# Making the second pair's operands in four stretches of the first pair instead of two

## The chip, the core and the metric

One program runs on 1 core of one Trainium2 chip. The metric is device time in microseconds (us) of that core, the median of repeated runs.

## The reference

One layer of a decoder trunk on 2048 tokens and 1024 features: a mixer (gated linear attention beside RWKV-7) added to the residual stream, then a channel mixer, then a final norm. The change lies in the channel mixer, `x2` being the residual stream after the mixer:

```python
h = modulate(x2, norm_ffn_g, sh_f, sc_f)         # rms norm, scale, shift
u = h @ w_up                                     # 1024 -> 2 * 2816
u = sum(conv_w[j] * up[:, j:j + T] for j in range(3)) + conv_b   # up: u with two zero rows ahead
gate, val = split(u, 2)
x = x2 + gt_f * ((silu(gate) * val) @ w_down)    # 2816 -> 1024
```

## The kernel before

The tokens are cut into four blocks of 512, and the channel mixer takes them in two pairs (`hs[0]`, `hs[1]`; loop variable `e`). The up projection of a pair goes over 22 tiles `j` of 128 gate features and the 128 value features beside them. A Strassen-Winograd scheme makes the four products of a tile out of seven smaller ones: seven `Up` slots a tile (`what` 1 to 7), each with 4 x 3 matmuls of 128x128 by 128x512 (L1296 to L1298; three, because each fp32 operand is carried as a rounded high part and a low part).

The moving operands of a pair are sums and differences of modulated quarters, named b11, b21, b22, t1 to t4, four tiles each. They are made once, written to DRAM (`opd`), and read back by `Feed`. For pair 0 that happens in the phase before. For pair 1 it happens while pair 0 runs its up tiles, in `made_ahead`:

- `operand_row` makes the row of inverse norms of a block with 4 small transposing matmuls (L1063) and one ScalarE copy (L1064).
- `operand_one(e, k)`, k = 0 to 3, loads two tiles of x2 (L1069), and its `rest` scales them (`op_scale`: VectorE L1073, ScalarE L1074) and stores b11 and b21 from ScalarE's queue (L1083).
- `operand_two(e, k)` loads two tiles of x2 and the b11 and b21 just stored. Its `rest` has two `op_scale`, two GpSimd subtractions (L1096, L1098), two VectorE operations (L1100, L1102), one store on ScalarE's queue (L1095) and four on SyncE's (L1097, L1099, L1101, L1103).

A step of `made_ahead` first runs the `rest` of the step before it and then issues its own loads; a last step, `None`, only runs the open `rest`. So `rest` of k runs one step after the loads of k. The tiles lie in a pool of five buffers (`acct`, tag "xt") that the down projection's accumulator tiles share.

Everything stands in one list of slots, which `run` goes through. A slot's weights are loaded six slots ahead and split into high and low part (`parts_of`: ScalarE L1217, then L1218 in turn on VectorE and GpSimd) three slots ahead; an `Other` slot counts in both distances. After each slot one background function is run: the convolution (`conv`, VectorE L1327 and L1328) and the gate (`hidden`, VectorE L1336, L1337, L1340) of the tile before. The matmuls of the down projection (`Down`, L1353 to L1355) come after every four up tiles, in 16 slots that stand behind slots 1 and 2 of tiles 3, 7, 11, 15, 19.

So PE runs in turn a stretch of 28 up slots (the last five of one tile, three whole tiles, the first two of the next) and a stretch of 16 down slots. The up stretches of pair 0 are called here S1 (tiles 4 to 6 whole), S2 (8 to 10), S3 (12 to 14) and S4 (16 to 18). Tile's scheduler gives each engine its fixed order at build time, from the program's order and a simulated clock; every engine then works through its queue in that order.

Of the kernel before, what the change touches and what calls it, by code (L numbers as in the profile page):

```python
# [95 lines left out]
def hybrid_kernel(ctx, tc, x, cst, vec, c_row, ada_t, w_in, w_v, w_first, w_z, gk_up, wa_up, g_up,  # L96
# [177 lines left out]
    step = [0]  # L274
# [235 lines left out]
    slots = (("rw_bk", 1), ("rw_rbk", 2), ("rw_rbk", 2), ("gl_g", 1), ("gl_vt", 1))  # L510
# [548 lines left out]
    def operand_row(b, at):  # L1059

        ps = pools["norm"]()
        for t in range(4):
            PE.matmul(out=ps[:, t * P:(t + 1) * P], lhsT=rn2[:, b, t:t + 1].broadcast_to([P, P]), rhs=ident, start=True, stop=True)  # L1063
        A.copy(out=at, in_=ps)  # L1064
        op_r[b] = at
# [170 lines left out]
    def bg_step():  # L1236
        if bg:
            bg.pop(0)()
        elif idle:
            idle.pop(0)()  # L1240
# [184 lines left out]
    def finish_later(b, sums):  # L1425
        r, rb = lp.tile([P, 4], F32, name="rn3", tag="rn3", bufs=2), []

        def norm():
            with tc.issue_after(state["last"]):
                rstd_tok(r, sum_tok(sums))  # L1430

        def rows():
            with tc.issue_after(state["last"]):
                rb.append(spread(up, r))

        def nothing():
            pass

        idle.extend([nothing] * 3 + [norm] + [nothing] * 2 + [rows])
        idle.extend(lambda ft=ft: finish_tile(b, ft, rb[0]) for ft in range(KT))  # L1440
# [3 lines left out]
    def down_slots(e, g, hid, sums=None, feed=()):  # L1444
        slots = []
        for ft in range(KT):
            shared = {}
            slots += [Down(e * HB + i, i, ft, g, hid, shared, sums, feed[ft * HB + i:ft * HB + i + 1]) for i in range(HB)]
        return slots
# [4 lines left out]
    def last_block():  # L1454

        wait = [Feed(0, n_, k, hs[0], cvt) for n_ in ("t2", "t3", "t1") for k in range(4)]
        gen = []

        def begin():
            at = iter(["b22"] * 4 + ["t4"] * 4)  # L1460
            pools["pair"] = lambda: hc(next(at))
            gen.append(stage_d(NBLK - 1, prep_d(NBLK - 1), lp.tile([P, NB], F32, name="d_ss", tag="fs", bufs=HB)))
            for f in wait[:2]:
                f.load()

        def one(ft):
            next(gen[0], None)
            for f in wait[2 * ft:2 * ft + 2]:
                f.split()
            for f in wait[2 * ft + 2:2 * ft + 4]:  # L1470
                f.load()

        def end():
            with tc.issue_after(state["last"]):
                for _ in gen[0]:
                    pass

        return [Other(begin)] + [Other(lambda ft=ft: one(ft)) for ft in range(KT)], Other(end)

    def made_ahead(e):  # L1480

        open_ = []

        def step(f):
            for r in open_:
                r()
            open_[:] = [f()] if f is not None else []

        def first(f, b):
            with tc.issue_after(state["last"]):  # L1490
                operand_row(b, up.tile([P, NB], F32, name="rbc", tag="ns", bufs=1))
            return f()

        zones = []
        for i, f in enumerate((operand_one, operand_two)):
            fs = [lambda k=k, f=f: f(e, k) for k in range(4)]
            fs[0] = lambda g=fs[0], b=2 * e + i: first(g, b)
            zones.append([Other(lambda f=f: step(f)) for f in fs + [None]])
        return zones

    hs = [{} for _ in range(NBLK // HB)]
# [4 lines left out]
    slots = []  # L1506

    def U(e, j, what, *feed):
        slots.append(Up(j, what, us[e][j], hs[e], hids[e][group_of[j]], feed))

    def feeds(e, n_, place):
        return [Feed(e, n_, k, hs[e], place) for k in range(4)]

    def begin(e):
        U(e, 0, 1, *feeds(e, "b11", acct if e else ubt))
        U(e, 0, 2, *feeds(e, "b21", acct if e else ubt))
        U(e, 1, 1)

    def stage_e(e):
        if e == 0:  # L1520
            begin(0)
            work, end = last_block()
            slots.extend(work)
        U(e, 0, 6)
        U(e, 1, 2)
        U(e, 0, 7)
        if e == 0:
            slots.append(end)
        U(e, 0, 5)
        U(e, 0, 3, *(feeds(e, "b22", acct) if e == 0 else ()))  # L1530
        U(e, 1, 6)
        U(e, 0, 4, *feeds(e, "t4", acct))
        U(e, 1, 7)
        U(e, 1, 5)
        more = e + 1 < len(hs)
        zones = made_ahead(e + 1) if more else [[], []]
        for j in range(2, NH):
            aside = zones[0] if 4 <= j < 7 else zones[1] if 8 <= j < 11 else []
            U(e, j, 1)
            U(e, j, 2)  # L1540
            if j > 1 and group_of[j - 2] != group_of[j - 1]:
                slots.extend(down_slots(e, group_of[j - 2], hids[e][group_of[j - 2]]))
            U(e, j - 1, 3)
            U(e, j, 6)
            if aside:
                slots.append(aside.pop(0))
            U(e, j - 1, 4)
            U(e, j, 7)
            U(e, j, 5)
            if aside:  # L1550
                slots.append(aside.pop(0))
        U(e, NH - 1, 3)
        U(e, NH - 1, 4)
        if more:

            begin(e + 1)
            last = kgroups[-1]

            def flush():
                while bg:  # L1560
                    bg_step()
                sums[e][:] = [lp.tile([P, NB], F32, name="x_ss", tag="fs", bufs=HB) for _ in range(HB)]

            sums[e] = []
            slots.append(Other(flush))
            fs = [f for n_ in ("t2", "t3", "t1", "b22") for f in feeds(e + 1, n_, ubt)]
            slots.extend(down_slots(e, last, hids[e][last], sums[e], fs))

            def later():
                for i in range(HB):  # L1570
                    finish_later(e * HB + i, sums[e][i])

            slots.append(Other(later))
# [3 lines left out]
    for e in range(len(hs)):  # L1577
        stage_e(e)
# [101 lines left out]
```

## Time and profile before

| | us |
|---|---|
| median of 3 runs | 2907.91 (2906.29 to 2908.95) |
| the profiled execution | 2900.88 |
| its span, first to last instruction | 2899.1 |
| PE / DVE / ACT / POOL busy | 95% / 71% / 45% / 38% of the span |

The profiled execution is one run; its own time is 1.8 us above its span. PE is TensorE's matmuls and PEld its weight loads, DVE is VectorE, ACT is ScalarE, POOL is GpSimd, SPq is SyncE's queue of DMA issues. Names in rows are those of the kernel's tiles; L1218 is line 1218. Matmuls overlap in the engine's pipe, so what one costs is read from the distance of starts.

### The profile page before, as it was taken

To read this page: it belongs to the slowest core of one execution; us is meant where nothing else is said; L and a number is where in the kernel's file an instruction comes from. 1 tells how busy PE (TensorE), PEld (TensorE's weight loads), DVE (VectorE), ACT (ScalarE), POOL (GpSimd) and SP (SyncE) were. 2 spreads that over 40 slices of the span, in tenths; PEclk is the share of its full clock that TensorE was granted. 3 is DMA by queue.
4 is the path that set the end of the run, shared out by engine and by line. 5 is a ranking of instruction groups with operands and counts; after the bars stand their busy time and mean duration, and the time that the engine had idled before them with its cause. 6 is when DMAs were issued, how large, how long until landed. Compare 5 with 4: busy or idle time off the path is not lost.

```text
span 2899.1 us, 54969 instructions
## 1 busy us (share of the span) xinstructions
PE 2745.4 (95%) x20296; PEld 2224.0 (77%) x20296; DVE 2058.9 (71%) x4090; ACT 1309.7 (45%) x2737; POOL 1087.6 (38%) x1147
## 2 busy tenths in 40 slices
PE   6989999999999999999899998999999899999997
PEld 5778777877787877777677786888878678888887
DVE  8357877766766667867557868668597777595777
ACT  4445335444454445554343534435264344253443
POOL 5224212312221223322345545536336545363441
PEclk9999989999999998988899999999999999999999
DMA  8988955545555566664875446442544734425243
GB/s 287 336 286 307 313 166 171 175 135 162 171 173 155 167 185 192 208 191 153 287 262 167 131 155 198 130 141 88 164 155 156 246 123 127 142 83 165 88 135 105
DMA packets 381965, 520.49 MB, mean 180 GB/s; under 512 B 82816, under 2 KB 155776, under 8 KB 381696
## 3 DMA queue, kind: packets, MB, share of 16 engines
q1 hardware_dynamic: 342960, 475.02, 51.4%
q10 hardware_dynamic: 38736, 41.95, 4.2%
q8 instruction: 160, 2.62, 0.4%
q14 instruction: 109, 0.89, 0.1%
HBM read 361.65 MB, written 155.19 MB: 178 GB/s over the span
## 4 chain that ended last, share of the span: by engine, by line
PE 39%; DVE 8%; DMA 5%; issue 2%; ACT 1%; POOL 1%; SPq 0%; DVEq 0%; ACTq 0%; POOLq 0%
PE g_bank L1298 7%; PE g_bank L1296 7%; PE g_bank L1297 7%; PE g_bank L1353 5%; PE g_bank L1354 5%; PE g_bank L1355 5%; DVE cv L1327 1%; DMA acc<-acc 1%; DVE cv L1328 1%; DVE w_lo L1218 1%; PE g_bank L283 1%; PE g_bank L282 1%; PE g_bank L281 1%; DVE acc L1422 1%; DMA mx<-mix 1%
## 5 line engine op out<-in xcount | busy, mean ns | idle before, releaser
L1298 PE MATMUL g_bank<-h_hi,w_lo 128*128 128x512 f32 x1232 | 479.7, 394 | 16.6 <-DVE w_lo L1218 14.2
L1296 PE MATMUL g_bank<-h_hi,w_hi 128*128 128x512 f32 x1232 | 484.8, 394 | 9.2 <-ACT w_hi L1217 4.2
L1297 PE MATMUL g_bank<-h_lo,w_hi 128*128 128x512 f32 x1232 | 484.1, 393 | 0.0
L1217 ACT CAST w_hi<-w_st 128x512 fp32r<-128x512 f32 (+1 forms) x396 | 238.1, 607 | 466.7 <-PE g_bank L1354 326.5
L1356 DVE SCALAR_TENSOR_TENSOR acc<-g_bank,mod,acc 128x512 f32<-128x512 f32 (+1 forms) x200 | 144.2, 728 | 236.1 <-PE g_bank L1355 216.8
L1218 POOL TENSOR_TENSOR w_lo<-w_st,w_hi 128x512 fp32r<-128x512 f32 x154 | 224.6, 1459 | 221.3 <-ACT w_hi L1217 220.7
L281 PE MATMUL g_bank<-h_hi,w_hi 128*128 128x512 f32 x736 | 299.8, 408 | 3.2 <-DVE rn L243 2.2
L283 PE MATMUL g_bank<-h_hi,w_lo 128*128 128x512 f32 x736 | 295.5, 402 | 0.0
L282 PE MATMUL g_bank<-h_lo,w_hi 128*128 128x512 f32 x736 | 295.4, 402 | 0.0
L1298 PEld LDWEIGHTS g_bank<-h_hi,w_lo 128*128 128x128 f32 x1232 | 234.0, 190 | 72.4 <-DVE w_lo L1218 19.4
L1296 PEld LDWEIGHTS g_bank<-h_hi,w_hi 128*128 128x128 f32 x1232 | 234.1, 190 | 62.4 <-ACT w_hi L1217 9.4
L1297 PEld LDWEIGHTS g_bank<-h_lo,w_hi 128*128 128x128 f32 x1232 | 233.9, 190 | 48.7
L1353 PE MATMUL g_bank<-hh,w_hi 128*128 128x512 f32 x640 | 251.9, 397 | 9.2 <-DVE acc L1356 7.2
L1354 PE MATMUL g_bank<-hl,w_hi 128*128 128x512 f32 x640 | 251.2, 394 | 0.0
L1355 PE MATMUL g_bank<-hh,w_lo 128*128 128x512 f32 x640 | 251.2, 394 | 0.0
L1218 DVE TENSOR_TENSOR w_lo<-w_st,w_hi 128x512 fp32r<-128x512 f32 (+1 forms) x242 | 193.9, 801 | 21.3 <-ACT w_hi L1217 21.1
L281 PEld LDWEIGHTS g_bank<-h_hi,w_hi 128*128 128x128 f32 x736 | 140.6, 191 | 37.0 <-DVE rn L243 3.0
L283 PEld LDWEIGHTS g_bank<-h_hi,w_lo 128*128 128x128 f32 x736 | 140.4, 191 | 31.5 <-DMA w_lo<-klo 1.0
L282 PEld LDWEIGHTS g_bank<-h_lo,w_hi 128*128 128x128 f32 x736 | 140.8, 191 | 28.0
L1353 PEld LDWEIGHTS g_bank<-hh,w_hi 128*128 128x128 f32 x640 | 119.6, 187 | 43.3 <-DVE acc L1356 9.9
L1355 PEld LDWEIGHTS g_bank<-hh,w_lo 128*128 128x128 f32 x640 | 119.8, 187 | 29.5
L1354 PEld LDWEIGHTS g_bank<-hl,w_hi 128*128 128x128 f32 x640 | 119.8, 187 | 28.9 <-DVE hl L1340 0.3
(352 smaller groups left out, 6096.4 us busy)
## 6 DMA issues: line engine op xcount, KB each, us to landing
acc<-acc SPq DMA_DIRECT2D x352, 256.0 KB, 3.1
w_hi<-khi SPq DMA_DIRECT2D x188, 256.0 KB, 3.4
w_lo<-klo SPq DMA_DIRECT2D x188, 256.0 KB, 3.7
w_st<-in_ffn_up SPq DMA_DIRECT2D x176, 256.0 KB, 3.0
w_st<-in_ffn_down SPq DMA_DIRECT2D x80, 256.0 KB, 2.8
khi<-w_hi ACTq DMA_DIRECT2D x68, 256.0 KB, 4.0
klo<-w_lo SPq DMA_DIRECT2D x68, 256.0 KB, 4.0
w_st<-in_ada_t SPq DMA_DIRECT2D x64, 256.0 KB, 4.6
```

Source lines behind the costliest of these rows:

```text
L281: PE.matmul(out=ps, lhsT=wh, rhs=hi, start=k == 0, stop=False)
L282: PE.matmul(out=ps, lhsT=wh, rhs=lo, start=False, stop=False)
L283: PE.matmul(out=ps, lhsT=wl, rhs=hi, start=False, stop=k == KT - 1)
L1217: A.copy(out=hi, in_=t)
L1218: eng.tensor_tensor(out=lo, in0=t, in1=hi.bitcast(F32), op=ALU.subtract)
L1296: PE.matmul(out=ps, lhsT=wh[:, c], rhs=hi, start=first and k == 0, stop=False, skip_group_check=True)
L1297: PE.matmul(out=ps, lhsT=wh[:, c], rhs=lo, start=False, stop=False, skip_group_check=True)
L1298: state["last"] = PE.matmul(out=ps, lhsT=wl[:, c], rhs=hi, start=False, stop=last and k == 3, skip_group_check=True).ins
L1353: PE.matmul(out=ps, lhsT=wh, rhs=hh, start=j == 0, stop=False)
L1354: PE.matmul(out=ps, lhsT=wh, rhs=hl, start=False, stop=False)
L1355: PE.matmul(out=ps, lhsT=wl, rhs=hh, start=False, stop=j == n - 1)
L1356: V.scalar_tensor_tensor(out=a_, in0=ps, scalar=mod[:, 40 + ft:41 + ft], in1=a_, op0=ALU.mult, op1=ALU.add)
```

## The change

`made_ahead` now gives four lists of steps in place of two: each operand's four `k` are cut into two halves, each with its own closing `None`. In the loop over tiles, one step a tile is taken, behind slot 6 of the tile before slot 4, in tiles 4, 5, 6 (operand one, k = 0 and 1), 8, 9, 10 (operand one, k = 2 and 3), 12, 13, 14 (operand two, k = 0 and 1) and 16, 17, 18 (operand two, k = 2 and 3). Before, two steps a tile were taken, behind slot 6 and behind slot 5: operand one in tiles 4, 5 and once in 6, operand two in 8, 9 and once in 10.

```diff
         for i, f in enumerate((operand_one, operand_two)):
             fs = [lambda k=k, f=f: f(e, k) for k in range(4)]
             fs[0] = lambda g=fs[0], b=2 * e + i: first(g, b)
-            zones.append([Other(lambda f=f: step(f)) for f in fs + [None]])
+            zones += [[Other(lambda f=f: step(f)) for f in part + [None]] for part in (fs[:2], fs[2:])]
         return zones
...
-        zones = made_ahead(e + 1) if more else [[], []]
+        zones = made_ahead(e + 1) if more else []
         for j in range(2, NH):
-            aside = zones[0] if 4 <= j < 7 else zones[1] if 8 <= j < 11 else []
+
+            aside = zones[j // 4 - 1] if zones and j >= 4 and j % 4 != 3 and j < 20 else []
...
             U(e, j, 5)
-            if aside:
-                slots.append(aside.pop(0))
```

## Rows read from the trace of the kernel before

**Rows 1.** The page's line of busy time, share and instructions of each engine.

```profile
PE 2745.4 (95%) x20296; PEld 2224.0 (77%) x20296; DVE 2058.9 (71%) x4090; ACT 1309.7 (45%) x2737; POOL 1087.6 (38%) x1147
```

**Rows 2.** Windows S1, S2, S3, S4: length, PE, PEld, DVE, ACT, POOL busy, clock, DMA, GB/s.

```profile
1577.00:1656.00 79.00, 75.53 (x331) 60.80 (x331) 71.56 (x88) 47.77 (x80) 49.79 (x45) 1.00 0.43 140
...
1701.00:1793.00 92.00, 83.53 (x348) 67.29 (x347) 84.87 (x94) 49.05 (x82) 63.67 (x55) 0.94 0.54 173
...
1837.00:1914.00 77.00, 77.00 (x341) 63.72 (x340) 69.14 (x84) 46.72 (x77) 49.63 (x48) 1.00 0.28 91
...
1958.00:2035.00 77.00, 76.75 (x339) 63.23 (x338) 68.63 (x81) 45.16 (x75) 46.09 (x48) 1.00 0.27 86
```

**Rows 3.** PE's timeline: first matmul of S2, first down matmul behind it; the same for S3.

```profile
1701.26 0.39 PE L1296 MATMUL g_bank<-h_hi,w_hi 128*128 128x512 f32 x1
...
1792.57 0.39 PE L1353 MATMUL g_bank<-hh,w_hi 128*128 128x512 f32 x1
...
1837.37 0.39 PE L1296 MATMUL g_bank<-h_hi,w_hi 128*128 128x512 f32 x1
...
1913.55 0.39 PE L1353 MATMUL g_bank<-hh,w_hi 128*128 128x512 f32 x1
```

**Rows 4.** PE's waits with their releasers, on the timeline: first in S1, two in S2.

```profile
1623.25 0.50 PE L1298 MATMUL g_bank<-h_hi,w_lo 128*128 128x512 f32 x1 [0.60 <-DVE w_lo L1218]
...
1750.13 0.50 PE L1298 MATMUL g_bank<-h_hi,w_lo 128*128 128x512 f32 x1 [1.07 <-DVE w_lo L1218]
...
1771.11 0.80 PE L1298 MATMUL g_bank<-h_hi,w_lo 128*128 128x512 f32 x1 [3.83 <-DVE w_lo L1218]
```

**Rows 5.** PE's waits in S2 (first row) and S4, in total: us, times, longest.

```profile
PE g_bank L1298 <- DVE w_lo L1218: 7.6, 3, 3.8
...
PE g_bank L1298 <- POOL w_lo L1218: 0.3, 1, 0.3
```

**Rows 6.** Windows of 4 us in S2, columns as in rows 2: the clock falls.

```profile
1753.00:1757.00 4.00, 3.42 (x14) 2.55 (x14) 4.00 (x4) 1.05 (x3) 4.00 (x4) 1.00 0.63 217
1757.00:1761.00 4.00, 1.29 (x4) 1.04 (x4) 4.00 (x3) 0.00 (x0) 3.85 (x3) 0.86 0.31 112
1761.00:1765.00 4.00, 4.00 (x14) 3.14 (x14) 3.65 (x5) 3.48 (x6) 2.27 (x3) 0.72 0.90 310
...
1773.00:1777.00 4.00, 4.00 (x11) 3.13 (x10) 4.00 (x7) 2.18 (x4) 2.44 (x2) 0.51 0.91 284
```

**Rows 7.** Groups by line: L1073 in S1; then S2's VectorE and GpSimd work of operand two.

```profile
L1073 DVE SCALAR_TENSOR_TENSOR acc<-acc,mod,rbc 128x512 f32<-128x512 f32 x8 | 7.4, 969 | 1.3 <-DMA acc<-x 1.3
...
L1073 DVE SCALAR_TENSOR_TENSOR acc<-acc,mod,rbc 128x512 f32<-128x512 f32 x8 | 8.9, 1126 | 0.0
...
L1100 DVE SCALAR_TENSOR_TENSOR acc<-acc 128x512 f32<-128x512 f32 x4 | 3.8, 950 | 1.2 <-POOL acc L1098 1.2
L1102 DVE SCALAR_TENSOR_TENSOR acc<-acc 128x512 f32<-128x512 f32 x4 | 3.8, 948 | 0.0
...
L1096 POOL TENSOR_TENSOR acc<-acc 128x512 f32<-128x512 f32 x4 | 6.7, 1667 | 4.8 <-ACT acc L1074 2.0 <-DMA acc<-op_b 1.8 <-PE g_bank L1298 1.0
L1098 POOL TENSOR_TENSOR acc<-acc 128x512 f32<-128x512 f32 x4 | 6.6, 1647 | 0.0
```

**Rows 8.** VectorE's timeline in S2: operand two's operations up to the first PE wait.

```profile
1730.71 2.06 DVE L1073 SCALAR_TENSOR_TENSOR acc<-acc,mod,rbc 128x512 f32<-128x512 f32 x3
...
1736.34 1.77 DVE L1100 SCALAR_TENSOR_TENSOR acc<-acc 128x512 f32<-128x512 f32 x1 [1.19 <-POOL acc L1098]
...
1740.02 0.68 DVE L1102 SCALAR_TENSOR_TENSOR acc<-acc 128x512 f32<-128x512 f32 x1
...
1744.31 1.77 DVE L1073 SCALAR_TENSOR_TENSOR acc<-acc,mod,rbc 128x512 f32<-128x512 f32 x1
```

**Rows 9.** The small matmuls of a row of inverse norms, PE's timeline, in S2.

```profile
1726.21 1.05 PE L1063 MATMUL rj_bank<-ident,rn 128*128 128x128 f32 x8
```

**Rows 10.** SyncE's queue: a wait in S2's end; first read of pair 1's operands.

```profile
SPq L1374 <- DMA op_t<-acc: 3.2, 2, 2.9
...
2083.07 1.39 SPq L1249 DMA_DIRECT2D acc<-op_b  x2
```

## The prediction

> **What bounds the kernel now.** I read the busy line first: PE is busy 95% of the span, so a gain can only come from time in which PE stands still or runs slowly [rows 1]. Then I cut pair 0 into its stretches. Without steps, in S3, 28 up slots last 1913.55 - 1837.37 = 76.2 us, or 2.72 a slot and 19.05 a tile. S2, the same slots with all of operand two, lasts 1792.57 - 1701.26 = 91.3 us [rows 3]. The windows show the same: PE is never idle in S3, idle 0.25 us in S4, 3.5 us in S1 (79 - 75.53), 8.5 us in S2 (92 - 83.53), where the granted clock is also only 0.94 on average [rows 2]. The reader should see DVE beside it: 85 of 92 us busy in S2, 72 of 79 in S1, and still 69 of 77 where no step runs. The waits say how this reaches PE: in S2, 7.6 us are for `w_lo`, the low half of a weight, made by DVE [rows 5]. DVE takes its queue in order, so a split stands behind the operands' work; it is put there three slots (8.2 us) before PE needs it, or two real slots (5.4 us) where an `Other` slot lies between. When DVE is later than this, PE stops. In S2 the clock also falls after such stops, to 0.51 in one window, which is the lower of its two levels (1.2 GHz of 2.4) [rows 6].
>
> **The change part by part.** No operation is added or dropped; 8 executions of `rest` change place, with their 24 loads and 28 stores.
>
> *What S2 gives back.* 91.3 - 76.2 = 15.1 us. The small matmuls of a row (at most 1.05 us [rows 9]) move with operand two to S3, so about 14.1 us is stall. It splits into 8.5 us idle and 0.06 x 92 = 5.5 us of clock [rows 2], which sums to 14.0. All of it is operand two's: S3 has everything else and no loss.
>
> *What S1 gives back.* 3.5 us [rows 2].
>
> *Two halves of operand one, now in S1 and S2.* A whole one is 8 DVE operations, 7.4 us [rows 7]; a half is 3.7 us, in two lots of 1.85, a tile apart. How much can DVE take before PE stops? In S1 PE first waited at 1623 us, after all 7.4 us; in S2 at 1749 us, after the first six operations, 2.06 + 1.77 + 0.68 + 1.77 = 6.3 us [rows 4, 8]. So some 6 us are carried by the lead of the splits, and 3.7 lies below it. Price 0; the upper bound is half of S1's loss each, 3.5 us together.
>
> *Two halves of operand two, now in S3 and S4.* In S2 the 16 DVE operations took 8.9 + 3.8 + 3.8 = 16.5 us and the 8 GpSimd ones 6.7 + 6.6 = 13.3 us [rows 7]: 4.1 and 3.3 us for one `rest`. The two of a half come 43.5 and 62.6 us into the stretch (16 and 23 slots of 2.72), 19 us apart. DVE has 77 - 69.1 = 7.9 us to spare in S3 and 8.4 in S4 [rows 2], so about 2 us a tile. At the second `rest` its lag is 4.1 - 2.0 + 4.1 = 6.2 us, just at the 6 us. To this may come the hold on GpSimd: L1100 waits for L1098, 1.2 us in the one case where DVE had no backlog [rows 7, 8]. Now most cases will be of that kind, 1.2 us a `rest`, and the lag becomes 8.6 us. So 0.2 to 2.6 us of stall a stretch from this side; S4 idles 0.25 us for a late split before anything is added, so there is no margin below [rows 2, 5], and I take 2.5 each, 5 in all. Bounds: 0 and half of what S2 loses each, 14.1 together. Behind S3 and S4 come down stretches, in which DVE has little to do and catches up.
>
> *Queues.* SyncE's queue gets the same loads and stores, in other stretches. DMA is busy 0.54 of S2, and only 0.28 and 0.27 of S3 and S4 [rows 2]: price 0. What is late next would be the x2 tiles: operand two holds four of the five "xt" buffers, now for a tile's length. The down slots need them at the end of S3 and S4, and the last `rest` stands in the same place ahead of them (slot 6 of the third tile) as in S2 now, where SyncE's wait for these stores came to 3.2 us [rows 10] and PE went on into the down matmuls at 1792.57 without a gap. Price 0. The later end is no trouble: the last `rest` would run at about 1958 + 63 = 2021 us, and the first read of these operands was issued at 2083 [rows 10].
>
> *Slots.* Slots behind slot 5 vanish from four tiles and six tiles of S3 and S4 get one; each shortens the lead of a split by 2.72 us while it lies between. That is part of the two bounds above. The empty list for pair 1 changes nothing.
>
> **A rule against the change.** Rows first: in S2 GpSimd worked 63.7 us against 49.6 in S3, yet DVE's other work took 84.9 - 16.5 = 68.4 us there and 69.1 in S3 [rows 2, 7]; 13 us more of GpSimd made the rest of DVE's work no longer. The Trainium skill, "SBUF — State Buffer", section "Who interferes with whom", says that a VectorE instruction with two SBUF inputs and a GpSimd one that reads SBUF exclude each other, the second blocking until the first is done. By that rule the subtractions would cost DVE time in S3 and S4 that spreading doesn't save; the rows just read don't show it.
>
> **The sum.** 14.1 + 3.5 - 5.0 = 12.6 us. From the profiled execution's 2900.9 us that gives 2888.3. That run lies 7.0 us under the median of the timed ones and below the fastest of them, so I put the same difference on the median: 2907.9 - 12.6 = 2895.3, say 2895.
>
> **The rivals.**
>
> *The stall goes along with the work (no change).* S1 lost 3.5 us on 7.4 us of added DVE time, 0.47 of it; S2 lost 14.1 on 16.5 + 13.3 = 29.8 us of DVE and GpSimd time, again 0.47. If that share is lost wherever the work is put, S1 to S4 lose 17.6 us as before: 2907.9. Against it: PE's waits begin only after 6 to 7 us have been added [rows 4, 8], which is a threshold and no share, and the clock's 5.5 us need long stops (3.8 us was the longest [rows 5]). For it: DVE is 90% busy in S3 and S4 without any step. If half of it were true the gain would be 9 us.
>
> *GpSimd's subtractions block DVE (slower).* In each of S3 and S4 DVE gets 8.2 us of its own and loses 6.6 us to the two pairs of subtractions, 14.8 in all, and has 7.9 and 8.4 us to take them: 6.9 + 6.4 = 13.3 us lost, and with stops of that length the clock's 5.5 us in both, 11. So 24.3 us against 17.6 saved: 2914.6. It decides once S3 and S4 lose over 11.7 us each (17.6 + 5.8, halved). For it: DVE operations of 0.7 us stretch to 1.77 beside GpSimd [rows 8]. Against it: S2's DVE sum, above. This is where that rule of the Trainium skill would lead.
>
> *The steps don't spread.* The order on each engine is fixed by the scheduler's clock and not by the program alone; if it draws the steps together, little changes: 2907.
>
> **How the numbers follow.** Forecast, S3 and S4 together losing 0 to 10 us: 0.68, with 2890 to 2900. Stall in proportion: 0.20, of which a quarter keeps a gain over 5.8 us and a tenth turns slower. Blocking: 0.08. No spreading: 0.04. Changes of 0.2% (5.8 us) are about what a measurement of this kernel can tell from none. So faster 0.68 + 0.05 = 0.73, same 0.13 + 0.04 = 0.17, slower 0.10. The 8-in-10 range starts at the price of nothing in S3 and S4, 2907.9 - 17.6 = 2890.3, less a microsecond of scatter, 2889, and goes up into the proportional case, to 2907.
>
> **What would show it.** Right: four up stretches of 77 to 80 us; DVE some 73 us busy in S1 and S2 and 77 in S3 and S4; PE without a wait in S1 and S2 and with 1 to 4 us in each of S3 and S4, for DVE's `w_lo`; a granted clock of 1.00 in all four. Wrong: S3 and S4 of 84 us and more with a fallen clock (proportion or blocking; in the blocking case DVE's other work is longer than 69 us), `rest` of two k close together, or a gap ahead of the down stretches with SyncE waiting for stores of the operands.

## The result, and the profile after

The changed kernel takes 2916.87 us (median of 17 executions; one of 5232.72 us stands apart, the others lie between 2909.70 and 2926.24). The kernel before, run beside it, takes 2901.56 (17 executions, 2893.22 to 2908.95). The ratio is 1.0051, 95% interval 1.0041 to 1.0062: the change costs 12 to 18 us. Forecast were 2895, with a range of 2889 to 2907, and a gain of 12.6; the result lies above the range, and the sign was wrong.

The profiled execution took 2920.11 us, its span 2918.3, which is 19.2 more than the span before. The page's busy line shows the same work as in [rows 1]:

```profile
PE 2750.0 (94%) x20296; PEld 2227.0 (76%) x20296; DVE 2066.5 (71%) x4090; ACT 1306.2 (45%) x2737; POOL 1087.2 (37%) x1147
```

The stretches S1 to S4, cut at the first up and the first down matmul of each, columns as in [rows 2]:

```profile
1581.67:1657.82 76.15, 73.61 (x321) 60.52 (x320) 71.90 (x87) 45.97 (x79) 50.09 (x46) 0.98 0.35 114
1702.62:1788.00 85.38, 79.30 (x338) 64.37 (x336) 72.59 (x86) 47.13 (x79) 46.98 (x48) 0.96 0.31 102
1832.80:1919.50 86.70, 80.08 (x345) 64.72 (x344) 78.26 (x92) 48.45 (x82) 57.26 (x52) 0.98 0.41 135
1964.30:2054.44 90.14, 80.89 (x338) 65.06 (x336) 77.22 (x93) 47.55 (x81) 57.31 (x52) 0.94 0.39 128
```

Two of S1's 28 slots run among the small down slots ahead of it, so S1 as cut here holds 26 and its length can't be set beside those of the others. S1 starts 1.9 us later than before (1579.82) and is 0.5 shorter; S2 falls from 91.3 only to 85.4, S3 grows from 76.2 to 86.7, S4 from 76.7 to 90.1. The four stretches sum to +17.5, and with the later start that is the whole difference of the two spans. S3 has VectorE's late splits, as the prediction named them, only more of them (6.2 us below). S2 and S4 are the odd ones. S2 holds half of operand one, which was priced at nothing; DVE is just as busy there as forecast (72.6 against "some 73"), and yet PE stands still for 6.1 us. So VectorE's load isn't the matter there. The waits (us, times, longest) say what is; PE, ACT and DVE in S2 first, then SyncE's queue from 1690 to 1716, then PE in S3 and in S4:

```profile
PE g_bank L1296 <- ACT ub L1305: 4.1, 1, 4.1
PE g_bank L1298 <- POOL w_lo L1218: 1.9, 1, 1.9
...
ACT acc L1074 <- DVE acc L1073: 13.7, 3, 8.4
...
DVE acc L1073 <- DMA acc<-x: 11.5, 4, 6.7
...
SPq L1069 <- DMA acc<-acc: 4.7, 3, 2.2
SPq L1069 <- DMA op_b<-acc: 3.5, 1, 3.5
...
PE g_bank L1298 <- DVE w_lo L1218: 6.2, 3, 2.6
...
PE g_bank L1298 <- DVE w_lo L1218: 3.8, 1, 3.8
PE g_bank L1298 <- POOL w_lo L1218: 2.7, 3, 1.8
PE g_bank L1296 <- ACT ub L1305: 2.7, 1, 2.7
```

VectorE stands 11.5 us for loads of x2, a wait that came to 1.3 us in S1 before [rows 7]; ScalarE stands 13.7 us behind VectorE; and PE waits 4.1 us for a copy that ScalarE makes (`ub`, L1305). SyncE's queue, which issues the loads (L1069), stands 4.7 us for the down slots' stores, whose buffers the loads fill, and 3.5 for a store of an operand made just before. The timeline at the start of S2 shows the chain link by link (SyncE's issues, VectorE, ScalarE, PE; the bracket is the idle time before and its releaser):

```profile
1698.52 0.38 SPq L1382 DMA_DIRECT2D acc<-acc  x1
...
1701.66 0.32 SPq L1069 DMA_DIRECT2D acc<-x  x1
...
1705.23 0.96 SPq L1069 DMA_DIRECT2D acc<-x  x2
1706.67 0.32 SPq L1382 DMA_DIRECT2D acc<-acc  x1
1710.54 0.32 SPq L1069 DMA_DIRECT2D acc<-x  x1
...
1704.66 1.33 DVE L1073 SCALAR_TENSOR_TENSOR acc<-acc,mod,rbc 128x512 f32<-128x512 f32 x1 [6.68 <-DMA acc<-x]
...
1714.23 0.75 DVE L1073 SCALAR_TENSOR_TENSOR acc<-acc,mod,rbc 128x512 f32<-128x512 f32 x1 [2.88 <-DMA acc<-x]
...
1706.02 0.73 ACT L1074 ACTIVATE acc<-acc,mod 128x512 f32<-128x512 f32 x1 [8.41 <-DVE acc L1073]
...
1715.02 0.72 ACT L1074 ACTIVATE acc<-acc,mod 128x512 f32<-128x512 f32 x1 [2.92 <-DVE acc L1073]
1715.65 0.57 ACT L1305 COPY ub<-g_bank 128x512 f32<-128x512 f32 x1
...
1717.47 0.58 ACT L1305 COPY ub<-g_bank 128x512 f32<-128x512 f32 x1
...
1713.58 0.39 PE L1298 MATMUL g_bank<-h_hi,w_lo 128*128 128x512 f32 x1
1718.10 0.79 PE L1296 MATMUL g_bank<-h_hi,w_hi 128*128 128x512 f32 x1 [4.14 <-ACT ub L1305]
```

A step's load (L1069) is issued among the stores of the down slots (L1382) whose "xt" buffers it fills. VectorE's L1073 waits for it, ScalarE's L1074 for that, and behind L1074 stand two copies out of PSUM, for the second of which PE stops behind the matmul of 1713.58. The loads of this step are hung on slot 6 of tile 8 and its `rest` on that of tile 9, within S2, which begins at 1702.62; on the chip the first load is issued at 1701.66, and VectorE stands at the `rest` from 1697.98 on (1704.66 - 6.68).

Why it is early shows in the order that the scheduler gave VectorE. Of VectorE's queue only the operands' operations and two markers are listed, from the start of S1 (u: an up slot's L1309; d: a down slot's L1356, d14 and d16 so many of them; O: L1073; P: L1100 or L1102). Added are three kernels of the experiments:

```
before    uuuOOOOOuOOuOuuuuuuu d16 uuuOOOuPPuOuOPPOuOPuPOuOPPuuu d16 uuuuuuuuuuuu d16 uuuuuuuuuuuu
after     uuuOOOOuuuuuuuuu d14OdOOdO uuuuuuuuuuuu d16 uuuOOOuPPuOuPPuuuuuu d14OdOdPPOO uPuPuuuuuuuuuu
e1_row    uuuOOOOuuuuuuuuu d16 uuuOOOOuuuuuuuuu d16 uuuOOOuPPuOuPPuuuuuu d16 uuuOOOuPPuOuPPuuuuuu
e2_pin    uuuuuuOOuuuOOuuu d16 uuuuuuOOuuuOOuuu d16 uuuuuuOOuPPuuOOPPuuu d16 uuuuuuOOuPPuuOOPPuuu
e4_unpin  OOOuOOOOuOuuuuuuuuuu d14OdOdPPOOuOPuPOuOuPPOuPuPuuuuuu d16 uuuuuuuuuuuu d16 uuuuuuuuuuuu
```

In the changed kernel the steps of S2 and S4 begin between the last two down slots, ahead of the stretch. Only the first step of an operand has something that holds it: `first` makes the row of inverse norms inside `tc.issue_after(state["last"])`, and every L1073 behind it reads that row. The second halves, k = 2 and 3, find the row ready, and the scheduler draws them as far forward as its clock allows. Also, the two `rest` of a half stand together (OOOO) and not a tile apart.

### The profile page after: what moved, and what is told of

Its sections match the earlier page's. It is cut to its first block, busy times and chain, and to the rows that moved or that the text cites. A ratio compares the mean times of both kernels' runs of the same rounds, so it can differ in the third digit from the quotient of the medians.

```text
span 2918.3 us, 54965 instructions
## 1 busy us (share of the span) xinstructions
PE 2750.0 (94%) x20296; PEld 2227.0 (76%) x20296; DVE 2066.5 (71%) x4090; ACT 1306.2 (45%) x2737; POOL 1087.2 (37%) x1147
## 4 chain that ended last, share of the span: by engine, by line
PE 36%; DVE 10%; DMA 6%; issue 2%; ACT 1%; POOL 1%; SPq 0%; DVEq 0%; ACTq 0%; POOLq 0%
PE g_bank L1298 7%; PE g_bank L1296 7%; PE g_bank L1297 7%; PE g_bank L1353 4%; PE g_bank L1355 4%; PE g_bank L1354 4%; DVE cv L1327 2%; DMA acc<-acc 1%; DVE cv L1328 1%; DMA acc<-x 1%; DVE w_lo L1218 1%; DVE hl L1340 1%; DVE acc L1422 1%; DVE th L1337 1%; PE g_bank L282 1%
## 5 line engine op out<-in xcount | busy, mean ns | idle before, releaser
L1296 PE MATMUL g_bank<-h_hi,w_hi 128*128 128x512 f32 x1232 | 485.8, 395 | 13.7 <-ACT ub L1305 7.1
L1217 ACT CAST w_hi<-w_st 128x512 fp32r<-128x512 f32 (+1 forms) x396 | 237.1, 606 | 450.6 <-PE g_bank L1354 333.3
L1356 DVE SCALAR_TENSOR_TENSOR acc<-g_bank,mod,acc 128x512 f32<-128x512 f32 (+1 forms) x200 | 144.3, 728 | 234.4 <-PE g_bank L1355 214.2
```

The source lines that it names most:

```text
L1217: A.copy(out=hi, in_=t)
L1296: PE.matmul(out=ps, lhsT=wh[:, c], rhs=hi, start=first and k == 0, stop=False, skip_group_check=True)
L1356: V.scalar_tensor_tensor(out=a_, in0=ps, scalar=mod[:, 40 + ft:41 + ft], in1=a_, op0=ALU.mult, op1=ALU.add)
```

## The experiments

All times are medians in us, each with the kernel before run on the same chip (2900.3 to 2902.2, beside e13 and e14 2906.4). The last column is the time from the start of S1 to the end of S4 in the one profiled execution, 455.25 for before and 472.77 for after; what lies outside those stretches varies between the profiled executions by some 20 us (2432 to 2453) and isn't in it.

| kernel | median (range) | ratio to before, 95% | S1 to S4 |
|---|---|---|---|
| e1_row | 2907.62 (2900.61 to 2917.61) | 1.0019, 1.0006 to 1.0033 | 459.30 |
| e2_pin | 2901.48 (2887.71 to 2909.92) | 1.0001, 0.9986 to 1.0015 | 454.55 |
| e4_unpin | 2907.70 (2904.86 to 2922.28) | 1.0032, 1.0019 to 1.0045 | 469.12 |
| e7_none | 2876.44 (2871.59 to 2879.42) | 0.9918, 0.9905 to 0.9931 | 436.08 |
| e3_bpin | 2903.19 (2896.93 to 2909.51) | 1.0006, 0.9991 to 1.0020 | 459.74 |
| e12_nosub | 2902.14 (2893.85 to 2912.17) | 0.9996, 0.9981 to 1.0010 | 452.54 |
| e10_slots | 2878.13 (2871.38 to 2885.80) | 0.9932, 0.9915 to 0.9948 | 437.10 |
| e9_noslot | 2896.28 (2886.61 to 2905.16) | 0.9990, 0.9975 to 1.0004 | 456.49 |
| e8_stage | 2888.84 (2881.48 to 2890.48) | 0.9967, 0.9954 to 0.9979 | 447.04 |
| e13_mul | 2891.71 (2881.68 to 2896.81) | 0.9945, 0.9925 to 0.9966 | 446.06 |
| e14_muladd | 2889.82 (2881.86 to 2900.25) | 0.9942, 0.9920 to 0.9963 | 445.40 |
| e15_pin3 | 2890.76 (2884.68 to 2895.23) | 0.9968, 0.9953 to 0.9983 | 447.52 |
| e16_cutv | 2899.04 (2887.75 to 2904.32) | 0.9992, 0.9977 to 1.0008 | 453.49 |
| e6_down | 2882.30 (2877.55 to 2892.46) | 0.9950, 0.9932 to 0.9967 | 442.99 |

### Is it the hold that the second halves lack?

**e1_row** gives k = 2 a row of its own, made again:

```diff
             fs[0] = lambda g=fs[0], b=2 * e + i: first(g, b)
+            fs[2] = lambda g=fs[2], b=2 * e + i: first(g, b)
```

> The changed kernel, with a row of inverse norms made afresh ahead of the third step of each operand too, so that all four half lists begin behind a matmul of their own place. Theory A (a half list without a fresh row is drawn by the scheduler into the down stretch ahead, and VectorE then waits for tiles that wait for buffers): no wait of L1073 for a load of x in S2 and S4, S2 falls from 85.4 us to about 81 and S4 from 90.1 to about 87, the whole to about 2909 (2904 to 2912), still not under the kernel before, since two steps still run in a bunch behind each row. Theory B (a fixed share of the added VectorE and GpSimd time is lost wherever it is put): no change from 2917, or slower by the two rows, 2 us.

It came to 2907.62. In the order above no step stands between down slots any more, and in the trace VectorE's L1073 waits for no load. The windows of S2 and S4:

```profile
1695.62:1775.06 79.44, 77.78 (x346) 63.65 (x345) 71.34 (x84) 47.77 (x80) 49.54 (x47) 1.00 0.35 110
...
1950.89:2035.58 84.69, 79.95 (x346) 64.77 (x345) 75.24 (x88) 47.42 (x80) 53.39 (x51) 0.98 0.42 134
```

S2 is 5.9 shorter, S4 5.5, S3 stays (86.23). So about 9 of the 15 us come from the missing hold (ratios 1.0051 and 1.0019).

**e4_unpin** takes the hold away in the kernel before:

```diff
-            with tc.issue_after(state["last"]):
-                operand_row(b, up.tile([P, NB], F32, name="rbc", tag="ns", bufs=1))
+            operand_row(b, up.tile([P, NB], F32, name="rbc", tag="ns", bufs=1))
```

> The kernel before, with the row of inverse norms made without being queued behind the last matmul (the two-stretch lists are as they were). Theory A: without that hold operand two goes into the end of the down stretch and VectorE waits there for x as in the changed kernel's S2 and S4, 10 us or so in all; S2 at 95 us or more, the whole slower than before by 5 to 15 us, 2911. Theory B: as before, 2901.6.

It is 0.32% slower (5.5 us), at the low end of theory A's range. Operand two now begins in the down stretch, and S2 takes 99.2 us against 91.3:

```profile
1708.85:1808.08 99.23, 83.68 (x338) 65.77 (x336) 86.54 (x101) 49.96 (x85) 63.05 (x56) 0.93 0.50 164
```

Giving the hold to the one kernel and taking it from the other moves both the way that this cause demands.

### What would the change bring if the steps stood where they are hung?

**e2_pin** holds each `rest` behind VectorE's last L1309 (`lastv`):

```diff
         def step(f):
             for r in open_:
-                r()
+                with tc.issue_after(state["lastv"]):
+                    r()
```

> The changed kernel, with each rest issued on VectorE behind the last L1309 of its own slot, so that one step a tile is what the queue really has. No operation is added. Theory A: no wait of L1073 for x, S1 and S2 at 77 to 78 us, S3 and S4 at 78 to 82, the whole at 2892 (2888 to 2898), faster than the kernel before: the place of the steps was right and the queue did not have it. Theory B: 2917 as the changed kernel, or 2901 as the one before, since the same work is added to the same stretches.

The order is now the one the prediction spoke of (OO, a tile, OO), and it is 15 us faster than the changed kernel. But it takes 2901.48, the same as before: the gain that the spread was expected to bring (2892) isn't there.

**e3_bpin** is the kernel before with the same hold, so two stretches with two steps a tile.

> The kernel before, two stretches and two steps a tile, with every rest pinned behind VectorE's last L1309, as in e2_pin. Theory E (spreading over four stretches has a worth of its own once the steps stay where they are hung): two stretches take what e2_pin's four take, but in bunches, so this one is slower than e2_pin's 2901.5 by 5 us or more: about 2908, with S2 at 90 us or more. Theory F (each step costs what it costs, some 25 us over the twelve, wherever it stands): 2899 to 2904, the same as before and as e2_pin, with S1 at 75 and S2 at 91.

2903.19 lies in theory F's range and 5 us under theory E's number. Its S2 takes 84.9, where theory E said 90 or more and theory F 91, and its S1 to S4 are 5.2 us longer than e2_pin's in the one execution of each. The medians differ by 1.7 us with intervals that overlap. Held in this way, four stretches are at best worth a few us more than two, not the 12.6 that were forecast.

**e7_none** measures what there is to gain: pair 1's operands aren't made at all.

```diff
-            nc.sync.dma_start(out=self.t, in_=opd[self.e][self.n_][self.k])
+            nc.sync.dma_start(out=self.t, in_=opd[0][self.n_][self.k])
...
-        zones = made_ahead(e + 1) if more else [[], []]
+        zones = [[], []]
```

> The kernel before without making the second pair's operands at all: the second pair reads the first pair's from DRAM, so its outputs are the first pair's products; all loads, matmuls and the rest stay. This is the floor for any placing of the steps. Both theories: S1 to S4 at 76.2 us each, the whole 17.6 us under the kernel before, 2884 (2881 to 2887). If it is well above, part of the stalls in S1 and S2 has another cause than the steps.

2876.44. The steps cost the kernel before 20 to 28 us by the interval, not the 17.6 of the prediction; S1 to S4 show 19.2 of it. The stretches without them:

```profile
1576.88:1647.62 70.74, 70.74 (x314) 58.58 (x313) 64.73 (x80) 42.36 (x72) 46.10 (x44) 1.00 0.27 86
1692.42:1769.26 76.84, 76.48 (x337) 62.98 (x336) 68.91 (x81) 45.11 (x75) 47.42 (x48) 1.00 0.27 86
1814.06:1890.97 76.91, 76.52 (x338) 63.00 (x336) 68.77 (x81) 45.02 (x75) 46.51 (x48) 1.00 0.27 85
1935.77:2012.96 77.19, 76.47 (x337) 63.01 (x336) 69.90 (x81) 45.13 (x75) 47.67 (x48) 1.00 0.27 86
```

A row's small matmuls take PE 0.8 us of these differences (from the first of them at 1599.34 to the next matmul at 1600.14 in S1 before). S2's loss of 14.1 was read rightly (91.3 - 76.8 - 0.8 = 13.7). S1 loses 5.1 (76.6 - 70.7 - 0.8) and not 3.5: only PE's idle time had been read there, since no stretch of its kind without steps was at hand.

### What takes the time in the spread kernel?

First the rival of the prediction. **e12_nosub** is e2_pin without the two subtractions on GpSimd for pair 1:

```diff
-            G.tensor_tensor(out=b11, in0=b11, in1=b12, op=ALU.subtract)
+            if e == 0: G.tensor_tensor(out=b11, in0=b11, in1=b12, op=ALU.subtract)
```

(and the same for L1098).

> e2_pin without GpSimd's two subtractions in pair 1's operand two (L1096, L1098 left out, so t1 to t4 of pair 1 hold other values). Theory G (GpSimd's subtractions hold VectorE up, the rival of the prediction): S3 and S4 lose their 13.3 us of it and their clock loss, down from 83 and 82 to 77 to 78 each, so 2901.5 - 11 = 2890 or less. Theory H (the steps cost through ScalarE's wait for L1073 and VectorE's own queue; GpSimd's work lies beside): S3 and S4 fall by 0 to 3 us each, 2896 to 2901, and S1 and S2 stay.

2902.14 against 2901.48: no gain, with intervals of about 4 us to either side, where theory G wanted 11 us. S3 and S4 fall by 1.9 and 0.6 us, to 81.4 and 81.7, not to 77 or 78. Theory G falls as it was priced; the median lies 1 us above the range of theory H.

**e10_slots** is e7_none with twelve empty `Other` slots, to see what the slots cost alone, and **e9_noslot** is e2_pin with the steps hung on slot 6, so that no `Other` slot shortens the lead of the splits.

> As e7_none (the second pair's operands are not made and the first pair's are read), with twelve empty slots where the changed kernel has its steps. The lead alone: if slots cost by themselves, S1 to S4 grow by 1 us or more each and the whole goes from 2876 to 2880 or more; theories A, C and D say 2876 to 2878.

> As e2_pin, with the steps hung on slot 6 in place of slots of their own, so that the weights are split a full three up slots ahead. If the shorter lead is what e2_pin still loses: 2893. Theories C and D: 2899 to 2902.

Empty slots cost 1.7 us with overlapping intervals, so nothing that can be told. e9_noslot came to 2896.28, 5 us under e2_pin, its interval reaching 1.0004 and overlapping e2_pin's: between the two expectations. Whether the slots' lead is worth something stays open. What e9_noslot keeps is ScalarE's wait.

**e8_stage** cuts `rest` into three parts (L1073; L1074; subtractions and the rest), hung on slots 6, 4 and 7 of a tile, and holds each behind the last own work of all three engines (`lasta`: ScalarE's copy L1305; `lastg`: GpSimd's split):

```diff
+                with tc.issue_after(state["lastv"]), tc.issue_after(state["lasta"]), tc.issue_after(state["lastg"]):
+                    open_[0][s_]()
...
+            slots[-1].aside = three[:1]
             U(e, j - 1, 4)
+            slots[-1].aside = three[1:2]
             U(e, j, 7)
+            slots[-1].aside = three[2:]
```

> As e2_pin, with each rest cut into three parts one slot or more apart (VectorE's scaling, then ScalarE's addition, then the rest), each part issued behind the last instruction of its slot on VectorE, ScalarE and GpSimd, and without slots of their own. Theory C (ScalarE and GpSimd stand at the head of their queues for the part before, as ScalarE did 6.3 us in each stretch of e2_pin, and the weights' splits stand behind): those waits fall under 1 us, S2 to 77, S3 and S4 to 79, the whole at 2890. Theory D: S2 at 79, S3 and S4 at 82 to 83, the whole at 2901 as e2_pin.

2888.84, 0.33% under before. That changes two things at once, the cut on VectorE and the hold on ScalarE and GpSimd. **e13_mul** and **e14_muladd** run two of the three parts together.

> e8_stage with its second and third part run together, two slots behind the first: L1073 alone, then L1074 and the rest. Theory K (what e8_stage gains over e9_noslot, 7.4 us, comes from ScalarE's L1074 no longer standing at the head of its queue while VectorE gets to L1073): this keeps it, 2887 to 2891. Theory L (it comes from VectorE's work standing in smaller bunches): operand one's bunch is as in e8_stage and operand two's is cut at the same place too, so 2887 to 2891 as well; the two are told apart by e14_muladd.

> e8_stage with its first and second part run together: L1073 and L1074 behind slot 6, the rest behind slot 7. VectorE's bunches are those of e8_stage; only ScalarE comes to L1074 early and waits again, some 25 us in all. Theory K (ScalarE's wait): the gain is lost, 2894 to 2898. Theory L (VectorE's bunches): it is kept, 2887 to 2891.

Both kept the gain, and e14_muladd's would speak for theory L. But it was no test of theory K: with the hold on ScalarE still in place, ScalarE's wait for L1073 did not come back (2.7 us in all). So the two were taken apart: **e15_pin3** has the hold without the cut (`slots[-1].aside = three` behind slot 6), **e16_cutv** the cut of e14_muladd without the hold on ScalarE and GpSimd:

```diff
-                with tc.issue_after(state["lastv"]), tc.issue_after(state["lasta"]), tc.issue_after(state["lastg"]):
+                with tc.issue_after(state["lastv"]):
```

> e8_stage with all three parts run together behind slot 6, as in e9_noslot: VectorE's bunches are e9_noslot's, but L1074 is pinned behind ScalarE's copy L1305 and the subtractions behind GpSimd's last split, as in e8_stage. Theory K (ScalarE stood at L1074 while its copies and roundings waited): 2887 to 2892, like e8_stage and e14_muladd. Theory L (VectorE's bunches): 2894 to 2899, like e9_noslot.

> e14_muladd, operand two's rest cut in two parts two slots apart, pinned on VectorE alone: ScalarE comes to L1074 early again. Theory K: 2894 to 2899, with ScalarE waiting some 25 us for L1073. Theory L: 2887 to 2892.

2890.76 and 2899.04, with intervals that just touch (up to 0.9983, from 0.9977). Both fall on theory K's side. Who waited for L1073 from S1 to S4 (us in all, times), in e15_pin3 and behind the dots in e16_cutv (L1076 is L1074 in both):

```profile
who waited for it (us, times):
  ACT acc L1076: 1.1, 2
...
  ACT acc L1076: 24.8, 12
```

e2_pin has 25.4 there, e9_noslot 26.3. In the listing used above, VectorE's orders of e15_pin3 and e16_cutv are the same to the letter (in operand two both have the subtractions' followers one slot later than e9_noslot, so e15_pin3 is set against e16_cutv here; of VectorE's other operations some change places); ScalarE's differ (w: a rounding L1217, c: a copy L1305, A: L1074; in S1):

```
e16_cutv  cwcwwwcwcwAAcwwcwwwcwcwAAcww
e15_pin3  wwcwcwwcwcAAwwwcwcwwcwcAAwww
```

In e16_cutv, as in e9_noslot, L1074 stands ahead of two copies that it follows in e15_pin3, and ScalarE waits for VectorE there while the copies and roundings queue behind it. How this comes back to PE can be followed in S2 (1697.00 to 1776.52 in e16_cutv, first rows; 1692.77 to 1769.62 in e15_pin3, behind the dots; lines 1229, 1230, 1340 and 1341 are 1217, 1218, 1326 and 1327 of the kernel before):

```profile
1741.89 0.72 ACT L1076 ACTIVATE acc<-acc,mod 128x512 f32<-128x512 f32 x1 [3.01 <-DVE acc L1073]
1745.21 0.82 ACT L1340 ACTIVATE cv<-ub,vt 128x512 f32<-128x512 f32 x1
1746.12 1.45 DVE L1341 SCALAR_TENSOR_TENSOR cv<-ub,vt,cv 128x512 f32<-128x512 f32 x1 [1.97 <-ACT cv L1340]
1757.51 0.50 PE L1312 MATMUL g_bank<-h_hi,w_lo 128*128 128x512 f32 x1 [1.52 <-DVE w_lo L1230]
...
1734.76 0.82 ACT L1340 ACTIVATE cv<-ub,vt 128x512 f32<-128x512 f32 x1
1737.28 1.34 ACT L1076 ACTIVATE acc<-acc,mod 128x512 f32<-128x512 f32 x2
1738.07 0.74 DVE L1341 SCALAR_TENSOR_TENSOR cv<-ub,vt,cv 128x512 f32<-128x512 f32 x1
```

In e16_cutv ScalarE's part of the convolution (L1340) stands behind the waiting L1076, VectorE's part (L1341) waits 1.97 us for it, and VectorE, busy 68.0 of the 79.5 us of S2, comes later to the split for which PE stops (58.7 us after the start of S2 against 57.1; there it falls beside an addition on GpSimd, 1755.31 to 1756.91, and takes 1.75 us against 0.68). In e15_pin3 L1340 runs ahead of L1076, VectorE doesn't wait for it, and PE has no wait in S2. So the cost runs from VectorE over ScalarE back to VectorE, over the convolution and not over the rounding alone. From S1 to S4 VectorE's wait for the convolution and PE's wait for `w_lo` are in e16_cutv (first two rows) and e15_pin3:

```profile
DVE cv L1341 <- ACT cv L1340: 21.3, 18, 3.2
PE g_bank L1312 <- DVE w_lo L1230: 9.0, 6, 3.0
...
DVE cv L1341 <- ACT cv L1340: 13.8, 12, 3.1
PE g_bank L1312 <- DVE w_lo L1230: 5.9, 3, 2.8
```

The other kernels with a step a tile go the same way: where L1073 keeps ScalarE waiting, 21.8 and 9.7 in e2_pin and 23.0 and 11.3 in e9_noslot; with the hold, 12.3 to 13.1 and 4.2 to 4.7 in e8_stage, e13_mul and e14_muladd. The holds on ScalarE and on GpSimd were not tried one without the other. But operand one has nothing on GpSimd, and 4.0 of the 6.0 us by which e15_pin3's S1 to S4 are shorter than e16_cutv's lie in S1 and S2 (73.5 and 79.5 against 72.1 and 76.9), where only operand one is made; there it is ScalarE's hold. In S3 and S4 e12_nosub, where GpSimd has nothing of operand two to do and nothing is gained, speaks for ScalarE's. The windows of e15_pin3:

```profile
1575.85:1647.97 72.12, 72.12 (x322) 59.23 (x320) 68.22 (x81) 44.50 (x76) 47.32 (x45) 1.00 0.34 114
1692.77:1769.62 76.85, 76.74 (x337) 62.85 (x336) 70.67 (x84) 47.00 (x79) 49.54 (x47) 1.00 0.36 113
1814.42:1894.54 80.12, 77.72 (x345) 63.82 (x344) 72.76 (x81) 45.89 (x77) 53.82 (x50) 1.00 0.36 122
1940.62:2023.37 82.75, 78.75 (x337) 63.99 (x336) 75.42 (x83) 45.46 (x76) 57.36 (x51) 0.98 0.40 130
```

S2 is back at the floor of e7_none (76.84), S1 1.4 above it, S3 and S4 3.2 and 5.6; of S1's and S3's the row is 0.8 each.

### A better place

**e6_down** hangs the steps among the down slots, where VectorE and ScalarE are little used, with tiles of other pools, so that no step waits for an "xt" buffer, and each `rest` held behind VectorE's last L1356. Its placing:

```diff
+        return {7: [(1, one[0], 3), (5, one[1], 3), (9, one[2], 3)], 11: [(1, one[3], 3), (6, two[0], 4)],
+                15: [(1, two[1], 4), (7, two[2], 4)], 19: [(1, two[3], 4)]}
```

(tile: down slot of the load, step, slots from there to its `rest`).

> The steps are taken out of the up stretches and put among the slots of the down stretches at tiles 7, 11, 15 and 19, three, two, two and one, each rest on VectorE behind the last L1356 of its slot; the tiles lie in two buffers of the sums and two of the up tiles that are free there, and not in the accumulators' five. Theory A (queue order and waits for buffers) and theory D (in an up stretch VectorE has no time to spare, so a step costs PE time wherever it stands in one, and in a down stretch VectorE is busy 18 of 45 us) both say: S1 to S4 at 76 to 78 us, down stretches 44.8 to 47, the whole at 2882 (2877 to 2888). If the down stretches grow by more than 3 us each, the 4 MB of transfers a stretch are the new limit.

2882.30, 0.50% under before and 6 us above e7_none: the lowest median and the shortest S1 to S4 of all that do the whole work. (By the ratio e13_mul and e14_muladd are level with it; the kernel before ran highest beside them.) ScalarE waits as long as in e2_pin, 26.9 us, but in the down stretches PE loses nothing by it; two of them:

```profile
1767.42:1813.35 45.93, 45.93 (x202) 37.02 (x201) 21.92 (x32) 8.66 (x15) 12.99 (x10) 1.00 0.70 224
1891.09:1935.89 44.80, 44.80 (x193) 35.91 (x192) 23.10 (x33) 8.36 (x14) 15.26 (x12) 1.00 0.76 252
```

PE is busy without a gap, ACT 8 to 9 us of 45 to 46. In the changed kernel steps ran in down stretches too and lost. There their loads waited for the down slots' buffers, and the `rest` had no hold; e6_down changes both, and one without the other was not tried.

## Why the prediction was wrong, point by point

**The step that failed** is that "8 executions of `rest` change place" to where the list hangs them: "16 and 23 slots", "19 us apart", "two lots of 1.85, a tile apart". The prediction's own rival "The steps don't spread" names the cause, with a chance of 0.04 and the price "little changes: 2907". Chance and price were both off: the scheduler did draw them together, and the kernel took 15 us more than before, since the second halves were drawn ahead of the start of their stretch, among the down slots. That the row's hold reaches only the first half was to be read in the diff and in `first`; e1_row and e4_unpin show what it is worth, some 9 and 5.5 us.

**"Price 0" for SyncE's queue and the "xt" buffers** looked at one direction alone, whether the down slots would find their buffers late. The steps' loads waited for the down slots' buffers instead, and VectorE 11.5 us for the loads in S2.

**The tolerance ("some 6 us are carried by the lead of the splits")** was read from VectorE alone and doesn't hold for a spread step as e2_pin runs it: halves of operand one, 3.7 us of VectorE time, cost S1 and S2 2.8 and 2.5 us over e7_none (0.8 of S1's is the row). The tolerance failed through ScalarE, whose queue the prediction never costed; with ScalarE's order mended (e15_pin3) they cost 1.4 and 0, and price 0 comes out nearly right. A sign of it stood in S2 before, in the row below that of [rows 5], which the prediction left out:

```profile
PE g_bank L1296 <- ACT ub L1305: 0.9, 1, 0.9
```

**Operand two in S3 and S4, 2.5 each.** In the changed kernel it cost 9.8 and 13.0 over e7_none, more than the bound of 14.1 together. In e2_pin it was 6.4 and 5.1, in e15_pin3 3.2 and 5.6. Without the row in S3, e15_pin3's are 2.4 and 5.6: there S3 is as forecast and S4 is 3 us more.

**S1, 3.5,** was mis-sized: 5.1 (e7_none, without the row). **S2, 14.1,** was right: 13.7.

**The rivals.** "The stall goes along with the work" forecast no change, which is where e2_pin and e3_bpin lie; but its measure, 0.47 of VectorE's and GpSimd's added time, is refuted by e12_nosub (15.6 us of GpSimd's work less, no gain) and e15_pin3 (the same work as e16_cutv and 8.3 us cheaper). Among the kernels with a step a tile, cost went along with ScalarE's standing at L1074. It is no measure for the others: the kernel before has 9.0 us of that wait and e1_row 5.2, and their steps, which stand in bunches, cost 26 and 31 us over e7_none. That the bunches on VectorE are the cause there was not tested. "GpSimd's subtractions block DVE" was no cause of the time in e2_pin, as e12_nosub shows; the changed kernel itself was not tried without them. The rule of the Trainium skill weighed there ("SBUF — State Buffer", section "Who interferes with whom") would have made them cost VectorE time; some of it is there (last section), but it did not decide the end.

The forecast of a gain of 12.6 us from before's 2901.6 would be 2889.0. e15_pin3, the same spread with both queues in the order that the prediction took for granted, runs at 2890.8. The sum described a kernel that the change did not make; part of that agreement is chance, as S1's term was 1.6 too small and S3's and S4's 3.0 together, and e15_pin3 has no slots of their own for the steps. Of the 28 us between 2889.0 and 2916.9, some 15 lie between e2_pin and the changed kernel (the steps' place) and some 11 between e15_pin3 and e2_pin (ScalarE's order, and whatever the slots and GpSimd's hold are worth).

## What to carry to other kernels

Where a scheduler fixes each engine's order, the place in a program's list is only a wish: read or print the order that results, on every engine that the moved work touches, and look for what holds each part, above all when a list is cut in two and only its head had a hold. Work hung into a slack engine's queue blocks whatever stands behind it from its first unmet wait on, so price the wait and not only the busy time, and hold a consumer on its own engine (ScalarE's L1074) until its producer is due. And look for the stretch where all the engines concerned have room, and give the work buffers of its own there: among the down slots a wait of 27 us on ScalarE left PE without a gap.

## What the runs showed of the hardware

GpSimd's subtractions do lengthen VectorE's work a little, which the prediction's argument from S2's sum had not shown. In the same stretch of time, which holds S3 and S4 but for 0.6 us of e12_nosub's S3, e2_pin (first fence) and e12_nosub (second) have:

```profile
1825.00:2036.00 211.00, 204.18 (x876) 166.11 (x875) 168.28 (x199) 98.53 (x165) 120.02 (x109) 0.98 0.47 148
```

```profile
1825.00:2036.00 211.00, 202.34 (x879) 163.48 (x879) 164.66 (x200) 97.86 (x165) 104.46 (x101) 1.00 0.48 147
```

Eight GpSimd instructions fewer, 15.6 us of its time, and VectorE is 3.6 us less busy with one instruction more. PE's time did not follow, as the medians show. VectorE's L1073 takes 1218 ns in the mean beside the subtractions and 1033 without them, L1100 1050 and 704. So by these rows the engines got into each other's way for about a quarter of GpSimd's time, and that was not what the end waited for.
